# Output projection of a transformer layer as seven block products: low parts of the weights on VectorE, weight sums during the last gates, residual and copies placed early

## The chip, the cores and the metric

The kernel runs on one core of a Trainium2 chip. The metric is the time of one execution on the device in microseconds (us). The engines are named as in the profile: PE (TensorE, matrix products), DVE (VectorE), ACT (ScalarE), POOL (GpSimd) and SP (SyncE, which here only issues DMA transfers). Each engine takes its instructions strictly in the order of its own queue; an instruction that waits holds all that stand behind it on that engine.

## What is computed

One layer over 1024 tokens of width 1024, with 256 context tokens: a modulation from the conditioning vector; a windowed attention (branch A) and a global one (branch B) of 8 heads each; two sigmoid gates; a merge and an output projection; a residual with layer norm; then a convolutional feed-forward block with a second layer norm.

```python
h = x * (1.0 + scale1) + shift1
proj = h @ w_in + b_in
g_a, g_b = split(sigmoid(proj[..., OFF_GA:]), 2)
merged = g_a * (o_a @ w_branch_a) + g_b * (o_b @ w_branch_b)
y = merged @ w_out                                    # the output projection
x = layer_norm(alpha * x + gate1 * y, ln1_g, ln1_b)   # layer norm 1
h = x * (1.0 + scale2) + shift2
u = conv3(h @ w_up) + conv_b
x = layer_norm(alpha * x + gate2 * ((silu(u_gate) * u_val) @ w_down), ln2_g, ln2_b)
```

All is float32. A matrix product is made of three: each operand is split into a high part (rounded to the format that TensorE multiplies) and a low part (the rest), and high x high, high x low and low x high are added up in PSUM (`mm3`, L89 to L92). ACT makes the high part mostly (L82), another engine the low one by a subtraction (L87).

## The kernel before

Tiles are feature-major: 128 features by 1024 tokens. The stages, in order of the profile: query projections, gates, key and value projections and modulation (to about 340 us); 32 attention units (16 of branch A, then 16 of branch B) with the branch A products filled in; the branch B products (tile b) with the merges; the output projection (tile y, 771 to 899 us); the up projection (u and after it the block products a to d); the down projection and layer norm 2.

**The seven block products.** The output projection is a 2 x 2 block product of w_out (transposed) with the merged activations, done with seven half-size products in place of eight. Their order is `WSEQ = 1, 2, 6, 7, 4, 5, 3`. Each product p has two groups g, and each group two halves a, so that `wprod(p, g)` (L1394) gives two results of 128 x 512, each of 4 x 3 matmuls; product 3 does its columns in two slices of 256. Products 2, 4 and 3 add onto the PSUM banks of products 1, 7 and 5 (`WFROM`), so they must wait until those banks have been read. Three PSUM tiles of two banks ("big") go round.

What follows each product:

- Product 1: ACT copies the four results to SBUF (wx, L1424).
- Product 2: DVE adds gate1 times the result onto the residual (`gacc`, L1381; z holds alpha * x); then `zadd` adds z and its square onto the running sums zs (L1218) and zq (L1219) from which layer norm 1 takes mean and variance.
- Product 6: DVE subtracts from wx (L1302), ACT scales the result twice (wy, wx, L1442 and L1443), and POOL adds it at three places (`gsum`, L1388): 12 additions in all.
- Products 7, 4, 5, 3: `gacc` again, and `zadd` where a tile is complete.

The statistics of the first 512 tokens (tile sta, L1250 and L1251) are multiplied in the midst of product 5, by a tick that counts matmul columns; the normalized tiles (B, ACT L1296, zo L1299) feed the up projection.

**Weights.** `wout_load(p)` (L1137) loads the two weight tiles of a product into the raw ring (tag "raw", three buffers; L1152), splits them with ACT and POOL into hwo and lwo, and puts these into one of two rings of four buffers: "w" for products 6, 4 and "wd" for 2, 7, 5; products 1 and 3 have slots of their own. The weights of products 5, 6, 7 and 3 are sums of blocks of w_out, kept in DRAM as wod[1] to wod[4]. They are formed by transfers alone: `wo_put` (L772, issued by SP) copies a block, `wo_acc` (L775, issued by POOL) adds another to it. Each moves 1 MB. A table, `wo_sums`, starts them behind gates: (f = 4) copies 1 and 3, (7) additions to 1 and 3, (9) copy of 1 to 2, (11) addition to 2, (12) copy of 2 to 4, (14) addition to 4. There are 16 gates in two halves each of 24 matmuls; gates 12 to 15 come last, right before the attention.

**Slots.** `ht(name)` takes the oldest free slot (4 KB a partition) from the list `hfree`, and `hput` gives slots back. A tile in a re-used slot waits for the last reader of the tile before it. In the kernel before, wx takes the slots of bT1_7 and bT0_3, the last tiles of the merge, and the first z tiles those of bT0_7 and of the m tiles that product 1 reads.

**The merges.** `merge(f)` (L1098) adds the two branches and splits the result into m; `mbuild(k)` (L1114) forms the differences (bT, L1118) and splits them into W6, W7, W4, W5. These run on DVE, ACT and POOL while TensorE does the branch B products, whose results DVE multiplies by the gate (L1177).

**Who sets the order.** From L1415 on the order on PE is that of the program. On the other engines, and on all in the branch B loop, a planner puts the instructions in order when the kernel is built, from its own estimates of cost and the dependencies; only the sections marked `manual_schedule` are exempt. So the order on DVE, ACT, POOL and SP can differ from the order of the text.

Of the kernel before, what the change touches and what calls it, by code (L numbers as in the profile page):

```python
# [13 lines left out]
P = 128  # L14
# [3 lines left out]
KT = 8  # L18
# [9 lines left out]
HALF = 512  # L28
# [41 lines left out]
def layer_kernel(  # L70
# [600 lines left out]
    def wd_sums(n, j0, j1):  # L671
        def a(r, c):
            return w_dn[c * NH + j0:c * NH + j1][:, :, 4 * r:4 * r + 4].rearrange("n p f q -> p n (f q)")

        def put(key, src, *more):
            tag = tokens.pop()
            t = dpool.tile([P, j1 - j0, HALF], F32, tag=tag, name=f"sd{key}_{j0}")
            for j in range(j0, j1):
                sd[key, j] = t[:, j - j0]
            sd[key] = t  # L680
            nc.sync.dma_start(t, src)
            adds.extend((t, m) for m in more)

        if n == 0:
            put(1, a(1, 0), a(1, 1))
            put(3, a(0, 0), a(1, 0))
        elif n == 1:
            put(2, sd[1], a(0, 0))
        else:
            put(4, sd[2], a(0, 1))  # L690
# [77 lines left out]
    def wo_block(f, c):  # L768
        return w_out[f:f + 4][:, :, 4 * c:4 * c + 4].rearrange("n p k q -> p n (k q)")

    def wo_put(n, src):
        nc.sync.dma_start(wod[n], src)  # L772

    def wo_acc(n, src):
        nc.gpsimd.dma_start(wod[n], src, accum_op=ALU.add)  # L775

    wo_sums = {4: lambda: (wo_put(1, wo_block(4, 0)), wo_put(3, wo_block(0, 0))),
               7: lambda: (wo_acc(1, wo_block(4, 1)), wo_acc(3, wo_block(4, 0))),
               9: lambda: wo_put(2, wod[1]), 11: lambda: wo_acc(2, wo_block(0, 0)),
               12: lambda: wo_put(4, wod[2]), 14: lambda: wo_acc(4, wo_block(0, 1))}  # L780

    sgp = [None]

    def gate(f, hf):
        ps = acc_tile(f"g{f}_{hf}")
        s = slice(hf * HALF, (hf + 1) * HALF)
        for k in range(KT):
            h, l = ready["g", f][k // 4]
            n = slice(k % 4 * P, (k % 4 + 1) * P)
            mm3(ps, (h[:, n], l[:, n]), (hT[k][0][:, s], hT[k][1][:, s]), k == 0, k == KT - 1)  # L790
        if done[0] < total:
            if hf == 0:
                pool, tag = sring[f % 2]
                sgp[0] = pool.tile([P, 2, HALF], F32, tag=tag, name=f"sg{f}", bufs=1)
            sg = sgp[0][:, hf]
        else:
            sg = ph1.tile([P, HALF], F32, tag="sg", name=f"sg{f}_{hf}", bufs=2)
        nc.scalar.activation(sg, ps, AF.Sigmoid, bias=bgc[:, f:f + 1])  # L798
        nc.scalar.dma_start(sgd[f][:, s], sg)
        if hf and f in wo_sums:  # L800
            wo_sums[f]()
        return sg

    queue = [qpost(1, t) for t in range(NT)]
# [188 lines left out]
    for u in range(nu + 1):  # L993
        vs, fs = [], []
        while vq and (vq[0] <= u - VL or vq[0] >= 16 or u >= 17):
            vs += units[vq.pop(0)].value_steps()
        ss = []
        if u < nu:
            ss = units[u].score_steps()
            if u + 2 < nu:  # L1000
                ss.append(units[u + 2].qprep)
        if u == 31:
            first = branch_steps(1, w_b, (0, 1), att, (nc.gpsimd, nc.gpsimd), (0,))
            first[0]()
        for hf, (u0, u1) in enumerate(FILL):
            if u == u0:
                fill += branch_steps(0, w_a, (hf,), att, (nc.gpsimd, nc.gpsimd))
                ends = [n * (u1 - u0) / len(fill) for n in range(len(fill))]
            if u0 <= u < u1:
                fs = [fill.pop(0) for e in ends if u - u0 <= e < u - u0 + 1]  # L1010
        if u < nu:
            ss = [units[u].context] + ss
        seq = []
        for lst, of, sp in ((ss, 0.0, SPAN[u >= 17]), (vs, VOFF, VSPAN), (fs, 0.0, 1.0)):
            for n, st_ in enumerate(lst):
                seq.append((of + sp * (n + 0.5) / len(lst), st_))
        for _, st_ in sorted(seq, key=lambda e: e[0]):
            st_()
        while adds:
            t, m = adds.pop(0)  # L1020
            nc.gpsimd.dma_start(t, m, accum_op=ALU.add)
        if u in DNS:
            wd_sums(*DNS[u])
        if u < nu:
            vq.append(u)
            done(units[u].br, units[u].i, units[u].g)
# [20 lines left out]
    wb = {}  # L1047
# [26 lines left out]
    def hsl(hf):  # L1074
        return slice(hf * HALF, (hf + 1) * HALF)
# [13 lines left out]
    mB, mT = {}, {}  # L1089
    wor = {}  # L1090

    def z_start(f, hf):
        z = zt_[f, hf] = ht(f"z{f}_{hf}", (P, 2, HALF))
        for a in (0, 1):
            nc.sync.dma_start(z[:, a], xT[f + 4 * a][:, hsl(hf)])
        nc.scalar.mul(z, z, ALPHA)

    def merge(f, parts=(0, 1)):  # L1098
# [37 lines left out]

    def wout_load(p, first=False):  # L1137
        pool, tag = ((wq, "w") if WSEQ.index(p) % 2 == 0 else (post, "wd"))
        own = p in (1, 3)
        for g in (0, 1):  # L1140
            if first:
                r = ht(f"rwo{p}_{g}", (P, 2, HALF))
                hput(f"rwo{p}_{g}")
            else:
                r = post.tile([P, 2, HALF], F32, tag="raw", name=f"rwo{p}_{g}", bufs=3)
            src = WSRC[p]
            if type(src) is int:
                src = wod[src][:, 2 * g:2 * g + 2]
            else:
                f, c = src[0] + 2 * g, src[1]  # L1150
                src = w_out[f:f + 2][:, :, 4 * c:4 * c + 4].rearrange("n p k q -> p n (k q)")
            nc.sync.dma_start(r, src)  # L1152
            if own:
                h, l = (ht(f"{a}wo{p}_{g}", (P, 2, HALF), R32) for a in "hl")
            else:
                h, l = (pool.tile([P, 2, HALF], R32, tag=tag, name=f"{a}wo{p}_{g}", bufs=4) for a in "hl")
            split(r, h, l, nc.scalar, nc.gpsimd)
            wor[p, g] = h, l

    for f in (0, 1):  # L1160
        merge(f)
    wb[2] = weight(w_b[2], "wb2", 8, he=nc.scalar, le=nc.vector, rtag=None)
    for f in range(2, KT):
        bT[1, f] = ht(f"bT1_{f}")
        nc.sync.dma_start(bT[1, f], sgd[KT + f])
        w = wb[f // 2]
        halves = [(0, 1)] if f < KT - 1 else [(0,), (1,)]
        for hs in halves:
            n = HALF * len(hs)
            b = bT[1, f][:, hs[0] * HALF:hs[0] * HALF + n]  # L1170
            ps = big(f"b1_{f}") if len(hs) == 2 else sml(f"b1_{f}_{hs[0]}")
            for j in range(4):
                k = (f % 2) * 4 + j
                for m, hf in enumerate(hs):
                    a = O[1, hf, 0, j // 2][:, j % 2], O[1, hf, 1, j // 2][:, j % 2]
                    mm3(ps[:, hsl(m)], (w[0][:, k], w[1][:, k]), a, j == 0, j == 3)
            nc.vector.tensor_tensor(out=b, in0=ps, in1=b, op=ALU.mult)  # L1177
            if len(hs) == 1:
                merge(f, hs)
        if len(halves) == 1:  # L1180
            merge(f)
        if f >= 4:
            mbuild(f - 4)
        if f == 3:
            hput("hwb1", "lwb1")
            wb[3] = weight(w_b[3], "wb3", 8, he=nc.scalar, le=nc.vector, rtag=None)
        if f == 5:
            wout_load(1, True)
    opool.release()

    post = tc.alloc_tile_pool(name="post", bufs=1, side="left", reuse_waits="tile")
# [190 lines left out]
                                       in1=zv(f, s), op0=ALU.mult, op1=ALU.add)  # L1382

    def zadd(f, s, first=False):
        ln_add(zv(f, s), zs, zq, s, first, f"a{f}_{s.start}", nc.vector, nc.vector if s.start and f < 4 else nc.gpsimd)

    def gsum(f, s, src):
        nc.gpsimd.tensor_tensor(out=zv(f, s), in0=zv(f, s), in1=src, op=ALU.add)  # L1388
# [24 lines left out]

    order = ctx.enter_context(ExitStack())
    order.enter_context(tc.manual_schedule(engines={mybir.EngineType.PE}))  # L1415
    def four(n):
        return [t[:, a] for t in [ht(f"w{n}{g}", (P, 2, HALF)) for g in (0, 1)] for a in (0, 1)]

    wx = four("x")
    h0, h1 = hsl(0), hsl(1)  # L1420
    wout_load(2)
    for g in (0, 1):
        for a, o in enumerate(wprod(1, g)):
            nc.scalar.copy(wx[2 * g + a], o)  # L1424
    hput(*[f"m{k}_0" for k in range(4)], *[f"{a}wo1_{g}" for g in (0, 1) for a in "hl"])
    for f in range(4):
        z_start(f, 0)
    wout_load(6)
    for g in (0, 1):
        for a, o in enumerate(wprod(2, g)):  # L1430
# [3 lines left out]
    wout_load(7)  # L1434
    wy = four("y")
    for f in range(4):
        z_start(f, 1)
    for g in (0, 1):
        for a, o in enumerate(wprod(6, g)):
            f = 2 * g + a  # L1440
            sub(nc.vector, wx[f], o, wx[f])
            nc.scalar.activation(wy[f], wx[f], AF.Identity, scale=modc[:, 20 + f:21 + f])  # L1442
            nc.scalar.activation(wx[f], wx[f], AF.Identity, scale=ngain[:, f:f + 1])  # L1443
            gsum(f + 4, h0, wy[f])
            gsum(f + 4, h1, wy[f])
            gsum(f, h1, wx[f])
# [616 lines left out]
```

## Time and profile before

| | us |
|---|---|
| median of 3 runs | 1572.74 |
| lowest, highest | 1570.32, 1573.7 |
| the profiled execution | 1571.2 |
| its span in the profile | 1569.4 |
| output projection, first to last matmul | 771 to 899 |
| last gate ends, attention begins | about 340 |

In the rows of the profile, L12 is line 12 of the kernel. `out<-in` names the tiles without their numbers. A timeline row gives the start, the time from the first start to the last end of the merged instructions, the engine, the line, the operation, its shape and count, and in square brackets how long the engine had stood idle and what ended that. A row of waits reads: who waited for whom, the sum in us, how many times, the longest. A group row gives the least, median and greatest duration in ns, and when the first and the last began. SPq is the queue of transfers that SP issues; its time is that of issuing, not of the transfer.

### The profile page before, as it was taken

The page shows a single profiled execution, that of the slowest core. Times are in us where ns is not written, and L with a number is a line of the kernel's source. Part 1 is how long each engine was busy: PE and PEld are TensorE (multiplying, and loading weights), DVE is VectorE, ACT ScalarE, POOL GpSimd, SP SyncE. Part 2 cuts the span into 40 slices and gives each one's busy share as a digit, 9 for nine tenths or more (in the row PEclk, how much of TensorE's full clock was granted, in tenths as well). Part 3 has the DMA queues.
Part 4 walks back from the last instruction along what each step waited for, and adds up shares of the span by engine and source line. Part 5 has one row for each costly group of instructions (what it writes and reads, how often), then busy time and mean ns, then how long its engine had stood idle before and what let it go on. Part 6 is the DMA issues. An engine that isn't in the chain of part 4 may idle for free.

```text
span 1569.4 us, 22114 instructions
## 1 busy us (share of the span) xinstructions
PE 1514.1 (96%) x7716; PEld 1264.0 (81%) x7716; DVE 1186.0 (76%) x1770; ACT 816.9 (52%) x1352; POOL 816.5 (52%) x754
## 2 busy tenths in 40 slices
PE   9999999999999999999985799999999999999997
PEld 7888877888988888887764798888888888888887
DVE  6676876638988787777944778888888888647884
ACT  5322222449987776665362673544444444435552
POOL 0356522427876777763587445666677664021121
PEclk9999999999999999999988899999999999999998
DMA  9778893313235576644252223233344446996721
GB/s 372 269 238 289 237 320 120 118 64 76 68 102 121 141 175 143 173 102 145 74 194 94 70 79 121 86 117 117 111 102 112 115 115 187 362 261 211 253 101 54
DMA packets 119264, 243.63 MB, mean 155 GB/s; under 512 B 13424, under 2 KB 28272, under 8 KB 119024
## 3 DMA queue, kind: packets, MB, share of 16 engines
q1 hardware_dynamic: 101808, 209.16, 39.7%
q0 software_dynamic: 12512, 24.38, 9.9%
q10 hardware_dynamic: 4832, 8.68, 1.5%
q8 instruction: 60, 0.98, 0.3%
q14 instruction: 52, 0.43, 0.1%
HBM read 190.98 MB, written 74.25 MB: 169 GB/s over the span
## 4 chain that ended last, share of the span: by engine, by line
PE 83%; DVE 4%; DMA 3%; ACT 3%; issue 3%; POOL 2%; SPq 0%; DVEq 0%; ACTq 0%; POOLq 0%
PE ptr L605 4%; PE p L90 4%; PE p L91 4%; PE p L92 4%; PE av L628 4%; PE av L629 3%; PE g L90 3%; PE g L91 3%; PE g L92 3%; PE s L497 3%; PE s L498 3%; PE b L90 2%; PE b L91 2%; PE a L91 2%; PE d L91 2%
## 5 line engine op out<-in xcount | busy, mean ns | idle before, releaser
L548 ACT ACTIVATE p<-p,nm 128x1280 f32<-128x1280 f32 (+2 forms) x128 | 139.8, 1093 | 6.6 <-DVE p L546 6.0
L617 DVE TENSOR_TENSOR ptl<-ptr,pth 128x512 fp32r<-128x512 f32 x195 | 128.1, 684 | 19.9 <-ACT pth L616 17.4
L87 DVE TENSOR_TENSOR ld<-rd,hd 128x1024 fp32r<-128x1024 f32 x77 | 95.6, 1257 | 53.0 <-ACT hd L82 49.3
L616 ACT CAST pth<-ptr 128x512 fp32r<-128x512 f32 x195 | 111.4, 590 | 30.1 <-PE ptr L605 28.1
L82 ACT CAST hd<-rd 128x1024 fp32r<-128x1024 f32 x77 | 79.7, 1047 | 88.7 <-PE p L92 62.5
L605 PEld LDWEIGHTS ptr<-identr,pb 128*128 128x128 f32 x944 | 96.3, 140 | 24.0 <-ACT pb L551 3.1
L605 PE MATMUL ptr<-identr,pb 128*128 128x128 f32 x944 | 107.5, 245 | 1.5 <-ACT pb L551 1.0
L90 PE MATMUL p<-hd 128*128 128x512 f32 x264 | 104.7, 397 | 0.0
L628 PE MATMUL av<-pth,VT 128*128 128x512 f32 x236 | 104.1, 441 | 0.2
L91 PE MATMUL p<-ld,hd 128*128 128x512 f32 x264 | 104.0, 394 | 0.0
L92 PE MATMUL p<-hd,ld 128*128 128x512 f32 x264 | 103.3, 391 | 0.0
L90 PE MATMUL g<-hh,whg 128*128 128x512 f32 x256 | 99.9, 390 | 0.0
L87 POOL TENSOR_TENSOR wlg<-wg,whg 128x512 fp32r<-128x512 f32 x32 | 43.7, 1375 | 108.1 <-ACT whg L82 108.1
L92 PE MATMUL g<-hh,wlg 128*128 128x512 f32 x256 | 99.7, 389 | 0.0
L91 PE MATMUL g<-hl,whg 128*128 128x512 f32 x256 | 99.6, 389 | 0.0
L629 PE MATMUL av<-ptl,VT 128*128 128x512 f32 x236 | 97.4, 413 | 0.2 <-DVE ptl L617 0.2
L546 DVE TENSOR_SCALAR_CACHE_REDUCE p<-s,cvt,nmc 128x1024 f32<-128x1024 f32 x64 | 84.2, 1317 | 5.2 <-PE s L498 5.2
L497 PE MATMUL s<-KL,q 128*128 128x512 f32 (+2 forms) x192 | 73.5, 384 | 1.4 <-DVE p L546 0.9
L798 ACT ACTIVATE sg<-g,bgc 128x512 f32<-128x512 f32 x32 | 22.0, 687 | 96.5 <-PE g L92 91.7
L498 PE MATMUL s<-KL,q 128*128 128x512 f32 (+2 forms) x192 | 71.9, 374 | 0.0
L82 ACT CAST wS<-s 128x512 fp32r<-128x512 f32 x76 | 45.4, 621 | 46.8 <-POOL s L1302 46.8
L82 ACT CAST wA<-ru 128x512 fp32r<-128x512 f32 x57 | 35.4, 621 | 63.3 <-PE d L92 35.3
(457 smaller groups left out, 4982.3 us busy)
## 6 DMA issues: line engine op xcount, KB each, us to landing
wml<-in_wmodT_dram SPq DMA_DIRECT2D x48, 512.0 KB
ru<-in_w_up_dram SPq DMA_DIRECT2D x38, 512.0 KB
rd<-td SPq DMA_DIRECT2D x55, 256.0 KB
rd<-sd SPq DMA_DIRECT2D x44, 256.0 KB
rd<-in_w_dn_dram SPq DMA_DIRECT2D x33, 256.0 KB
wm<-in_wmodT_dram SPq DMA_DIRECT2D x16, 512.0 KB
wg<-in_w_g_dram SPq DMA_DIRECT2D x32, 256.0 KB
sgd<-sg ACTq DMA_DIRECT2D x32, 256.0 KB
```

The source lines that it names most:

```text
L82: nc.scalar.copy(hi, src)
L87: lo_eng.tensor_tensor(out=lo, in0=src, in1=hi.bitcast(F32), op=ALU.subtract)
L90: nc.tensor.matmul(ps, a[0], b[0], start=start, stop=False, skip_group_check=resumed)
L91: nc.tensor.matmul(ps, a[0], b[1], start=False, stop=False, skip_group_check=resumed)
L92: nc.tensor.matmul(ps, a[1], b[0], start=False, stop=stop, skip_group_check=resumed)
L497: nc.tensor.matmul(o, self.q[0][:, hs], ks, start=True, stop=False)
L498: nc.tensor.matmul(o, self.q[1][:, hs], ks, start=False, stop=stop)
L548: nc.scalar.activation(row, row, AF.Exp, bias=self.nm[:, hs], scale=-1.0, accum_out=self.sm[:, hs])
L605: i = nc.tensor.transpose(tr[:, h * P:(h + 1) * P], self.bits[:, h, n * P:(n + 1) * P], identr)
L617: nc.vector.tensor_tensor(out=lo, in0=tr, in1=hi.bitcast(F32), op=ALU.subtract)
L628: nc.tensor.matmul(self.av, v, hi, start=first, stop=False)
L629: nc.tensor.matmul(self.av, v, lo, start=False, stop=self.left == 0)
```

## The change

- The table of weight sums is keyed by gate and half. Copies 1 and 3 go behind gate (12, 0), the additions to them behind (13, 1), the copy of 1 to 2 behind (14, 1), the addition to 2 behind (15, 1). The copy of 2 to 4 goes behind attention unit 1, and the addition to 4 is put on the list that POOL issues at the end of unit 3.
- The split weights of the branch B products 2 and 3 (wb2, wb3) take slots of the free list; product 1's split weights then use the ring "w".
- wx takes its slots before the branch B loop: those of rwb1 and wf1 (counted out by the free list).
- The loads of the first four z tiles are issued in and after the branch B loop (`z_load`). Their slots are then those of hwb2, lwb2, lwb3 and bT0_3. The scaling by alpha (`z_scale`) stays where it was for the first half of the tokens, and for the second half goes into the loop of product 6.
- All 14 low parts of the output weights are made by DVE in place of POOL.
- In the second half of the tokens, the sums zs of f = 4 to 7 are added by DVE in place of POOL (the first, f = 4, is a copy and stays on POOL).

```diff
-    wo_sums = {4: lambda: (wo_put(1, wo_block(4, 0)), wo_put(3, wo_block(0, 0))),
-               7: lambda: (wo_acc(1, wo_block(4, 1)), wo_acc(3, wo_block(4, 0))),
-               9: lambda: wo_put(2, wod[1]), 11: lambda: wo_acc(2, wo_block(0, 0)),
-               12: lambda: wo_put(4, wod[2]), 14: lambda: wo_acc(4, wo_block(0, 1))}
+    wo_sums = {(12, 0): lambda: (wo_put(1, wo_block(4, 0)), wo_put(3, wo_block(0, 0))),
+               (13, 1): lambda: (wo_acc(1, wo_block(4, 1)), wo_acc(3, wo_block(4, 0))),
+               (14, 1): lambda: wo_put(2, wod[1]), (15, 1): lambda: wo_acc(2, wo_block(0, 0))}
...
-        if hf and f in wo_sums:
-            wo_sums[f]()
+        if (f, hf) in wo_sums:
+            wo_sums[f, hf]()
...
+        if u == 1:
+            wo_put(4, wod[2])
+        if u == 2:
+            adds.append((wod[4], wo_block(0, 1)))
...
-    def z_start(f, hf):
+    def z_load(f, hf):
         z = zt_[f, hf] = ht(f"z{f}_{hf}", (P, 2, HALF))
         for a in (0, 1):
             nc.sync.dma_start(z[:, a], xT[f + 4 * a][:, hsl(hf)])
+
+    def z_scale(f, hf):
+        z = zt_[f, hf]
         nc.scalar.mul(z, z, ALPHA)
...
-        own = p in (1, 3)
+        own = p == 3
...
-            split(r, h, l, nc.scalar, nc.gpsimd)
+            split(r, h, l, nc.scalar, nc.vector)
...
-    wb[2] = weight(w_b[2], "wb2", 8, he=nc.scalar, le=nc.vector, rtag=None)
+    def four(n):
+        return [t[:, a] for t in [ht(f"w{n}{g}", (P, 2, HALF)) for g in (0, 1)] for a in (0, 1)]
+
+    wb[2] = weight(w_b[2], "wb2", 8, tag=None, he=nc.scalar, le=nc.vector, rtag=None)
+    wx = four("x")
...
+        if f == KT - 1:
+            hput("hwb3", "lwb3")
...
-            wb[3] = weight(w_b[3], "wb3", 8, he=nc.scalar, le=nc.vector, rtag=None)
+            wb[3] = weight(w_b[3], "wb3", 8, tag=None, he=nc.scalar, le=nc.vector, rtag=None)
         if f == 5:
+            hput("hwb2", "lwb2")
             wout_load(1, True)
+        if f == 6:
+            z_load(0, 0)
+            z_load(1, 0)
+    z_load(2, 0)
+    z_load(3, 0)
...
-        ln_add(zv(f, s), zs, zq, s, first, f"a{f}_{s.start}", nc.vector, nc.vector if s.start and f < 4 else nc.gpsimd)
+        ln_add(zv(f, s), zs, zq, s, first, f"a{f}_{s.start}", nc.vector, nc.vector if s.start else nc.gpsimd)
...
-    hput(*[f"m{k}_0" for k in range(4)], *[f"{a}wo1_{g}" for g in (0, 1) for a in "hl"])
+    hput(*[f"m{k}_0" for k in range(4)])
     for f in range(4):
-        z_start(f, 0)
+        z_scale(f, 0)
...
     for f in range(4):
-        z_start(f, 1)
+        z_load(f, 1)
     for g in (0, 1):
         for a, o in enumerate(wprod(6, g)):
             f = 2 * g + a
             sub(nc.vector, wx[f], o, wx[f])
+            z_scale(f, 1)
```

More of the change, by code (lines that the diff above doesn't have):

```diff
@@ L1415, in layer_kernel @@
     order.enter_context(tc.manual_schedule(engines={mybir.EngineType.PE}))
-    def four(n):
-        return [t[:, a] for t in [ht(f"w{n}{g}", (P, 2, HALF)) for g in (0, 1)] for a in (0, 1)]
-    wx = four("x")
     h0, h1 = hsl(0), hsl(1)
```

## The prediction

> **What bounds the kernel now.** First the busy times on the page, then the view of who waited for whom, for TensorE alone.
>
> ```profile
> PE 1514.1 (96%) x7716; PEld 1264.0 (81%) x7716; DVE 1186.0 (76%) x1770; ACT 816.9 (52%) x1352; POOL 816.5 (52%) x754
> PE y L90 <- DVE z L1381: 12.8, 3, 5.8
> PE sta L1250 <- POOL zs L1218: 11.4, 1, 11.4
> PE y L90 <- ACT wx L1424: 9.5, 1, 9.5
> PE accka L91 <- DVE wlka L87: 4.0, 2, 2.1
> PE sta L1251 <- DVE zq L1219: 0.8, 1, 0.8
> ```
>
> TensorE is the bound: it is busy 96% of the span, so a change pays only where TensorE stands still or runs slowly. The second column of the waits is the sum in us. Four of the five rows belong to the output projection (tile y, statistics sta): 12.8 + 11.4 + 9.5 + 0.8 = 34.5 us. The fifth, 4.0 us, lies far earlier, in the key and value projection (accka). Next, time windows (length, busy times, granted clock, DMA share, GB/s).
>
> ```profile
> 220.00:240.00 20.00, 17.86 (x72) 14.27 (x71) 7.71 (x15) 2.45 (x4) 1.16 (x1) 0.91 0.94 287
> 240.00:260.00 20.00, 18.14 (x73) 14.55 (x72) 11.35 (x34) 5.82 (x12) 6.19 (x6) 0.91 0.37 117
> 320.00:340.00 20.00, 20.00 (x96) 16.55 (x96) 0.00 (x0) 4.06 (x12) 0.21 (x1) 1.00 0.14 53
> 760.00:780.00 20.00, 20.00 (x90) 16.57 (x89) 17.85 (x20) 8.34 (x14) 10.68 (x7) 1.00 0.30 100
> 771.00:899.00 128.00, 93.56 (x413) 78.49 (x411) 73.44 (x94) 65.06 (x92) 86.83 (x54) 0.84 0.38 128
> ...
> L90 PE MATMUL y<-m,hwo x64: 278/389/795, 771.5 to 899.4; 128*128 128x512 f32 x32, 128*128 128x256 f32 x32
> 794.03 0.43 PE y L91
> 797.30 0.23 PE y L91
> ```
>
> The projection occupies 771 to 899 us (its group row: first and last start). TensorE is busy 93.56 of these 128, so 34.4 us are idle, the four waits again. The last two lines, from the chain of work, show a second loss: just after the wait for wx a matmul takes 0.43 us, 3 us later 0.23. Six products of 48 full matmuls and one of 96 half-width ones make 336 full ones, and 336 x 0.23 = 77.3 us. So 128 - 77 = about 51 us are lost: 34.4 idle, some 16 to slow matmuls and the statistics' small ones. In 220 to 260 us TensorE issues 72 + 73 = 145 matmuls where 760 to 780 has 90 in 20 us: 35 too few, at 20/90 = 0.222 us each 7.8 us.
>
> **The change, part by part.** The sum is made against the profiled execution, 1571.2 us (span 1569.4); the median of the three times shown, 1572.74, is 1.5 above it.
>
> *Product 2.* ACT, POOL and DVE around the 9.5 us wait:
>
> ```profile
> 790.19 0.62 ACT L82 CAST W<-bT 128x512 fp32r<-128x512 f32 x1 [3.59 <-POOL bT L1118]
> 790.83 1.07 ACT L1424 COPY wx<-y 128x512 f32<-128x512 f32 x2
> 784.67 2.59 POOL L87 TENSOR_TENSOR lwo<-rwo,hwo 128x1024 fp32r<-128x1024 f32 x1 [2.19 <-ACT hwo L82]
> 788.45 1.71 POOL L1118 TENSOR_TENSOR bT<-bT,bT 128x512 f32<-128x512 f32 x1
> 783.77 0.69 DVE L87 TENSOR_TENSOR m<-bT,m 128x512 fp32r<-128x512 f32 x1
> 803.95 1.41 DVE L1381 SCALAR_TENSOR_TENSOR z<-y,modc,z 128x512 f32<-128x512 f32 x2 [8.44 <-ACT z L1096]
> ```
>
> Product 2 accumulates onto product 1's banks and must wait until wx has been copied out. Product 1 ends about 782.5 (771.5 + 48 x 0.23), but the copy stands on ACT behind a cast that waits for POOL's subtraction at 788.45, which stands behind the low part lwo. The change takes lwo off POOL, and gives wx slots that were free long before (those of rwb1 and wf1, where before they were the last bT tiles'). What is late next: the last m (783.77 + 0.69 = 784.5), then lwo of product 2, now on DVE. Where it is put first, product 2 starts about 786; behind the two or three low parts of W still to come, about 788. I take 4.5 us left of 9.5: **5 saved** (ends 0 and 9.5 plus 2 for the slow start). The z tiles, which came 8.44 us late for DVE at 803.95, must come earlier too, and do: three of the first four load into slots free before product 1 ends (hwb2, lwb2, lwb3), the last waits for bT0_3 until about 793, and is needed at about 798. Nothing is charged.
>
> *The low parts.*
>
> ```profile
> L87 POOL TENSOR_TENSOR lwo<-rwo,hwo x14: 2346/2400/3396, 746.0 to 847.1; 128x1024 fp32r<-128x1024 f32 x14
> L87 DVE TENSOR_TENSOR lwu<-rwu,hwu x6: 1214/1294/3377, 847.2 to 939.6; 128x1024 fp32r<-128x1024 f32 x6
> ACT hwo L82 <- DMA rwo<-wo: 17.6, 2, 9.5
> ```
>
> POOL loses 14 x 2.40 = 33.6 us, DVE takes 14 operations of lwu's shape: between 1.21 and, beside a busy POOL, 3.38 (the 847.18 row below). I take 1.22, because POOL's own lwo, beside which the 3.38 was measured, is gone. That makes 17.1 us, 14.6 of them after 771, where DVE is busy 73.4 of 128 us; they fit. The two of product 1 fall into 740 to 771, where DVE has about a tenth free. Their raw tiles now take the slots of hwb1 and lwb1, free about 750, 21 us before product 1: nothing charged; without that slack a late m would add 2.4 us to the wait of product 2.
>
> *Product 4 and the first statistics.*
>
> ```profile
> 835.78 1.27 POOL L1388 TENSOR_TENSOR z<-z,wx 128x512 f32<-128x512 f32 x1
> 836.76 0.47 PE L90 MATMUL y<-W,hwo 128*128 128x512 f32 x1 [4.07 <-DVE z L1381]
> 816.98 22.75 SPq L1152 DMA_DIRECT2D rwo<-wo  x4
> 841.74 15.67 SPq L1369 DMA_DIRECT2D rwu<-in_w_up_dram  x5
> 847.18 3.38 DVE L87 TENSOR_TENSOR lwu<-rwu,hwu 128x1024 fp32r<-128x1024 f32 x1 [9.25 <-ACT hwu L82]
> 853.82 1.40 DVE L1381 SCALAR_TENSOR_TENSOR z<-y,ngain,z 128x512 f32<-128x512 f32 x2
> 854.71 3.47 POOL L1218 TENSOR_TENSOR zs<-zs,z 128x512 f32<-128x512 f32 x2 [1.35 <-DVE z L1381]
> 858.23 0.59 PE L1250 MATMUL sta<-onec,zs 128*128 128x1 f32 x2 [11.41 <-POOL zs L1218]
> ```
>
> Product 4's second group waits for product 7's last additions, and these for the twelve gsum additions on POOL (12 x 1.27 = 15.2 us), with low parts between them. Without these the sums end some 20 us after product 6 begins (12 matmuls, 2.8, and two short operations, 1.5, before the first, then 15.2), while product 7 ends 22 us after: the wait goes, **4 saved, and 2 of slow clock** (ends 0 and 6). The statistics' wait is a chain: the raw ring has three buffers, freed by POOL's low parts, so SP spreads four loads over 22.75 us; rwu goes out only at 841.74, DVE stands 9.25 us for its cast, and the additions of product 4, queued behind lwu, run at 853.8. Product 4 ended about 842 (836.8 + 24 x 0.23): rwu went out at its end. With the ring freed by DVE it can go out once product 5's weights are split, some 3 us after product 4 begins. What is late next is the plain chain: an addition 0.70, zs on POOL 1.7, against 2.8 us of matmuls before the statistics; I leave 4 us for DVE's queue. Of 12.2 us **8 are saved, and 2** of the slow clock behind (ends 0 and 16).
>
> *Product 3 and the sums of the second half.*
>
> ```profile
> 880.12 1.47 DVE L1218 TENSOR_TENSOR zs<-zs,z 128x256 f32<-128x256 f32 x1 [1.16 <-POOL zs L1218]
> 883.24 0.58 PE L90 MATMUL y<-m,hwo 128*128 128x256 f32 x1 [5.84 <-DVE z L1381]
> 894.51 0.39 PE L90 MATMUL y<-m,hwo 128*128 128x256 f32 x1 [2.91 <-DVE z L1381]
> ```
>
> Three full zs additions go from POOL (1.7) to DVE (0.69, as the m row of that shape). That ends DVE's wait for POOL at 880.12, but here DVE also has the normalization of the first half. 5.84 + 2.91 = 8.75 us of waits: **2 saved**; and since the stage shortens in front of a DVE and ACT load that does not, **3 lost** before the up projection (ends +6 and -6).
>
> *The weight sums.* Before, they run behind gates 4 to 14; the last copy goes out at 222.80.
>
> ```profile
> 222.80 0.51 SPq L772 DMA_DIRECT2D wo<-wo  x1
> 230.20 1.28 DVE L194 CUSTOM_DVE_ANT_0 wml<-wml,scc,bmc 128x1024 f32<-128x1024 f32 x1 [7.33 <-DMA wml<-in_wmodT_dram]
> 232.15 0.50 PE L91 MATMUL accka<-wlka,hh 128*128 128x512 f32 x1 [2.14 <-DVE wlka L87]
> DMA to landing us min/median/max: 11.4/14.2/24.8
> 340.59 0.20 POOL L543 TENSOR_SCALAR p<-sinkb 128x4 f32<-128x4 f32 x1 [2.58 <-PE g L92]
> ```
>
> DVE stood 7.33 us for a modulation weight queued behind a sum's 1 MB copy; wlka came late, and TensorE stopped. The change takes 8 MB of copies and sums out of this stretch, whose DMA share is 0.94. The loss there was 7.8 us: **6 saved** (ends 0 and 7.8). They reappear with the last gates, which end about 340 (p waited for their last matmul); a half gate is 24 matmuls, 5.4 us, so the first copies go out about 302, the first additions about 318, the next copy about 329, where the DMA share is 0.14. POOL's addition into sum 2, due at 340, waits for that copy, and the copy for the first additions; queued behind it are POOL's preparations for the attention (p at 340.59). At the landing of 14.2 the additions land about 333 and the copy about 347: **1 lost**, after some cover (ends 0 and the slower rival below). The last sum goes to attention units 1 to 3: SP's copy stands ahead of query loads, POOL's issue ahead of the next units; nothing charged, as the cover is one unit.
>
> **The sum.** 5 + 6 + 10 + 2 - 3 + 6 - 1 = **25 us**: 1571.2 - 25 = 1546.2, and 1.5 more for the median: **1548**.
>
> **The skill's rule on the clock.** The Trainium skill, "TensorE: Matmul & The Clock Gate" (What's actually happening), says that the clock halves only after an idle window of about 3.4 us. By that rule, waits shortened to 1 to 3 us would cost no slow matmuls, and the sum would be about 3 us better (the better side below holds that). The trace disagrees: the window with the wait of 2.14 us at 232.15 has a clock of 0.91 and 18 matmuls too few, twice what 2.14 us hold.
>
> **The rivals.**
>
> *A, DVE becomes the bound.* For: DVE would have 73.4 + 14.6 + 2 = 90 us of work in the stage, and if each of the 12 low parts also meets a POOL addition (1.27), 105 us, against the 103 that I leave. If the low parts also stand in DVE's queue where ACT's casts waited 17.6 us for loads, the evictions stand with them, and the stage takes 105 + 18 = 123: 5 saved there, 6 - 1 early, 10 in all: 1563. Against: POOL loses the 2.40 us operations, and the loads come earlier as the ring is freed earlier. The Trainium skill, "SBUF — State Buffer" (Who interferes with whom), speaks for A: a VectorE operation with two SBUF inputs and a GpSimd one that reads SBUF exclude each other for a whole instruction. The trace agrees, lwu taking 3.38 us beside POOL's lwo and 1.21 at the least. By that rule each gsum blocks a low part as lwo blocked lwu.
>
> *B, the change doesn't do what it says:* additions on POOL still come last, loads still come late, and TensorE waits as before. For: 12 x 1.27 us of gsum stay. Price 0, with +-3: 1572. Against: the copies' and the ring's chains above both lead through lwo.
>
> *C, slower: POOL's queue stands at the start of the attention.* If each sum and copy lands in the longest time shown, 24.8 us, the additions land at 343, the copy at 368, and POOL's queue stands from 340.6 to 368; TensorE runs out after some 5 us: 22 lost; SP's copy into sum 4 then waits until 393 and holds queries: some 12 more. 34 - 25 = 9 slower: 1582. It decides from landings of about 22 us. Against: 24.8 was measured at a DMA share near 1.
>
> **Chances.** Forecast (1540 to 1556) 0.52; the better side (1533 to 1540, the slow clock and the statistics all won) 0.12; A (1556 to 1567) 0.22; B 0.06; C 0.08. The range 1533 to 1566 leaves out B, C, and little at the ends. What a measurement here tells from no change is 0.2%, 3 us: faster 0.86, same 0.06, slower 0.08.
>
> **What the profile after would show.** Right: TensorE's wait for wx under 5 us, its wait for zs under 5, no wait for wlka; lwo on DVE near 1.22; the stage near 105 us. A: waits of y for DVE's z above 15 us and lwo above 2. C: a wait of TensorE for POOL near 345 us. The forecast falls if low parts standing for casts hold the evictions on DVE, or the up projection waits for B tiles.

## The result and the profile after

The kernel after takes 1560.22 us (median of 4 executions, 1559.57 to 1562.15) against 1573.22 us for the kernel before beside it (4 executions, 1570.32 to 1575.53): a ratio of 0.992, 95% interval 0.9901 to 0.9939. It is faster by 0.8%, 13 us where 25 were forecast. The profiled execution took 1560.66 us, with a span of 1558.7 us, 10.7 us less than before.

The first view is again TensorE's waits (who waited for whom: sum in us, times, longest).

```profile
PE y L90 <- DVE z L1399: 8.7, 2, 5.1
PE accqa L90 <- ACT whqa L82: 8.4, 1, 8.4
PE y L90 <- ACT wx L1438: 6.0, 1, 6.0
PE sta L1268 <- POOL zs L1236: 4.0, 1, 4.0
```

Three rows belong to the output projection; with a fourth of 0.8 us (the zq row in the next timeline) they make 19.5 us where there were 34.5. The wait for wlka is gone. But a wait stands here that the kernel before did not have: accqa, a query projection, for 8.4 us. It is the only one of these rows whose place the change does not seem to touch.

Windows of time (length, busy times with counts for PE, PEld, DVE, ACT, POOL, then granted clock, DMA share, GB/s) show both ends of the account.

```profile
220.00:240.00 20.00, 20.00 (x90) 16.57 (x89) 18.29 (x34) 6.34 (x11) 0.34 (x1) 1.00 0.76 268
240.00:260.00 20.00, 20.00 (x90) 16.57 (x89) 7.33 (x19) 5.97 (x12) 5.23 (x6) 1.00 0.33 99
777.00:889.00 112.00, 92.60 (x417) 78.52 (x416) 87.18 (x108) 64.22 (x91) 59.03 (x39) 0.88 0.39 132
```

From 220 to 260 us TensorE now has 90 matmuls in each 20 us, where it had 72 and 73: the loss beside the weight sums is gone from there. The output projection takes 112 us where it took 128. And yet it starts later: the first matmuls of the stages, from the groups of each tile, stand so (us):

| | before | after |
|---|---|---|
| accqa, first to last | 88.9 to 110.4 | 88.8 to 121.6 |
| accka, first to last | 219.4 to 254.2 | 230.9 to 257.8 |
| last gate matmul | 340.0 | 343.7 |
| attention (s), first | 340.6 | 344.2 |
| output projection (y), first | 771.5 | 776.7 |
| up projection (u), first | 899.9 | 888.8 |

From y to u the kernel gained 128.4 - 112.1 = 16.3 us; up to y it lost 5.2. The rest (0.4) lies behind u. So 11.2 us were lost at accqa, 7.9 won at accka, and 1.6 lost during the attention.

What stood in front of accqa is seen in SP's queue and around it (start, time of issuing). The first fence has SP alone, the second POOL, ACT and PE.

```profile
77.30 0.63 SPq L772 DMA_DIRECT2D wo<-in_w_out_dram  x1
...
84.53 0.57 SPq L772 DMA_DIRECT2D wo<-in_w_out_dram  x1
99.86 0.52 SPq L772 DMA_DIRECT2D wo<-wo  x1
100.47 1.76 SPq L711 DMA_DIRECT2D wqa<-in_w_qa_dram  x3
...
122.75 0.50 SPq L772 DMA_DIRECT2D wo<-wo  x1
```

```profile
87.31 1.38 POOL L775 DMA_DIRECT2D wo<-in_w_out_dram  x1 [11.61 <-DMA wo<-in_w_out_dram]
110.37 0.62 ACT L82 CAST whqa<-wqa 128x512 fp32r<-128x512 f32 x1 [18.06 <-DMA wqa<-in_w_qa_dram]
111.04 0.80 PE L90 MATMUL accqa<-whqa,hh 128*128 128x512 f32 x1 [8.45 <-ACT whqa L82]
```

These are the weight sums. The text puts their entries behind gates 12 to 15, which end after 300 us; SP issues all four copies, the one named behind unit 1 too, between 77 and 123 us. The copy of sum 1 to sum 2 must wait for the addition that POOL issued at 87.31, so SP issues nothing between 85.10 (84.53 + 0.57) and 99.86: 14.8 us (the view of SP's waits puts 14.7 us of waiting to L772, 12.8 of it in one piece, all for transfers into wo). The last three wqa loads stand behind it, ACT's cast waits 18.06 us for them, and TensorE 8.45, with slow matmuls behind.

### The profile page after: what moved, and what is told of

Its sections match the earlier page's. It is cut to its first block, busy times and chain, and to the rows that moved or that the text cites. A ratio compares the mean times of both kernels' runs of the same rounds, so it can differ in the third digit from the quotient of the medians.

```text
span 1558.7 us, 22131 instructions
## 1 busy us (share of the span) xinstructions
PE 1515.0 (97%) x7716; PEld 1265.4 (81%) x7716; DVE 1207.3 (77%) x1787; ACT 817.5 (52%) x1352; POOL 780.6 (50%) x737
## 4 chain that ended last, share of the span: by engine, by line
PE 85%; DVE 5%; DMA 3%; issue 3%; ACT 2%; POOL 2%; SPq 0%; DVEq 0%; ACTq 0%; POOLq 0%
PE ptr L605 5%; PE p L90 4%; PE p L91 4%; PE p L92 4%; PE av L628 4%; PE av L629 3%; PE g L90 3%; PE g L92 3%; PE g L91 3%; PE s L497 3%; PE s L498 3%; PE b L90 2%; PE c L90 2%; PE a L91 2%; PE d L91 2%
```

## Experiments

Ratios are against runs of the kernel before on the same chip, with 95% intervals. Two theories stood at the outset. **Theory 1:** the late start of the output projection comes from the weight sums, because the planner issues them early; a copy depends on no gate, and the text's place is no dependency. **Theory 2:** the sums are harmless, and another edit (slots, early z loads) delays the work before y.

### The sums alone: sums_old and before_sums

sums_old is the kernel after with the old table; before_sums is the kernel before with only the new one.

```diff
# sums_old
-    wo_sums = {(12, 0): ..., (13, 1): ..., (14, 1): ..., (15, 1): ...}
+    wo_sums = {(4, 1): ..., (7, 1): ..., (9, 1): ..., (11, 1): ..., (12, 1): ..., (14, 1): ...}
-        if u == 1:
-            wo_put(4, wod[2])
-        if u == 2:
-            adds.append((wod[4], wo_block(0, 1)))
```

> The changed kernel with the table of weight sums of before (behind gates 4 to 14), all else as changed. Theory 1 (the planner is free to issue the sums once their table entries lie behind the marked section, and issues them at 77 to 130 us, where SP stands for the additions and the query weights come late): TensorE's wait for whqa (8.4) goes, the two waits for wlka (4.0 in all) come back, the first product of y starts at 771.5 as before and not at 776.7, and the time is 1560.2 - 5.2 = 1555. Theory 2 (the late start of y comes from other edits, through new slots or another order): the wait for whqa stays at 8, y starts at 776 to 777, the time is 1560.

> The kernel before with nothing changed but the table of weight sums (and the two entries in the attention units). Theory 1: a wait for whqa of about 8, none for wlka, y starts at 776.7, the projection takes its 128 us, the time is 1573.2 + 5.2 = 1578, slower than before. Theory 2: no wait for whqa, and 1573.

sums_old took 1558.83 us (0.9898, 0.9876 to 0.9921), before_sums 1576.1 us (1.0014, 1.0003 to 1.0025). TensorE's wait in before_sums:

```profile
PE accqa L90 <- ACT whqa L82: 8.8, 1, 8.8
```

The wait at accqa comes with the new table alone and goes with it. The attention's end moves too: y starts at 775.1 us in before_sums against 771.5, and at 773.3 in sums_old against 776.7 after. So the new table costs 2 to 4 us where it was to gain 5; by its times alone before_sums is 2.3 us slower than the kernel before (0.5 to 3.9 by the interval). Each start is that of one profiled execution, and y starts anywhere from 768.8 to 774.7 us in the six kernels with the old table; the last gate matmul parts the runs better: 337.3 to 341.3 us in those six, 343.5 and 343.7 with the new table. Theory 2 falls, though neither time is exactly what theory 1 gave (1555 and 1578): the waits of accka in the profiled run of sums_old (6.5 us, where the kernel before had 4.0) are part of the difference.

### The sums where the text puts them: sums_held

Each copy and each addition gets a dependency on the sigmoid of the gate that the table names, or on unit 1.

```diff
+    hold = [None]
     def wo_put(n, src):
-        nc.sync.dma_start(wod[n], src)
+        i = nc.sync.dma_start(wod[n], src)
+        if hold[0]:
+            tc.add_manual_dep(i.ins, hold[0], data, reason="held")
...
-        nc.scalar.activation(sg, ps, AF.Sigmoid, bias=bgc[:, f:f + 1])
+        hold[0] = nc.scalar.activation(sg, ps, AF.Sigmoid, bias=bgc[:, f:f + 1]).ins.name
```

> The changed kernel, in which each copy and addition also depends on the sigmoid of the gate (or on the unit) behind which the table names it, so that the planner can't issue it earlier. Theory 1: neither a wait for whqa nor for wlka, y starts at 771.5 - 7.8 = 764 unless the attention's start loses something; the time is 1547 to 1549, what the prediction's sum gave. Theory 2: y at 776, 1560. The prediction's rival C: TensorE waits at about 345 us because POOL's queue stands for the addition into sum 2; 2 us at the median landing, up to 30.

It took 1560.01 us (0.9911, 0.9887 to 0.9934): no better than the kernel after. The early part did what was expected: no wait for whqa or wlka, and the last gate matmul at 332.2 us, 7.8 earlier than before. But the attention then took 384.8 us (332.8 to 717.6) against 373.4, so the 1547 to 1549 us of theory 1 did not come. Its beginning, in two views (a window with the columns above, then POOL's and PE's timelines):

```profile
360.00:370.00 10.00, 3.97 (x22) 3.35 (x21) 2.66 (x5) 3.18 (x8) 5.87 (x9) 0.69 0.30 65
```

```profile
333.64 1.15 POOL L779 DMA_DIRECT2D wo<-in_w_out_dram  x1 [19.72 <-ACT sg L803]
...
352.93 1.16 POOL L1026 DMA_DIRECT2D wo<-in_w_out_dram  x1 [0.91 <-DMA wo<-wo]
363.43 0.72 POOL L647 TENSOR_TENSOR ot<-ot,rb 128x256 f32<-128x256 f32 x1 [5.21 <-DMA rb<-dn]
364.50 0.75 PE L605 MATMUL ptr<-identr,pb 128*128 128x128 f32 x4 [3.65 <-ACT rb L574]
```

TensorE is busy 3.97 of 10 us there, where the kernel before had 9.62. POOL does not stand for the sums themselves (0.91 us at 352.93), so that half of rival C does not happen. SP's queue does stand, in two places (two rows of its waits within 328 to 480 us; the last number is the longest wait):

```profile
SPq L579 <- DMA dn<-rb: 17.7, 12, 6.6
SPq L774 <- DMA wo<-in_w_out_dram: 4.7, 1, 4.7
```

The second row is the copy into sum 4, which waits for the addition into sum 2; the second q transfer stands behind it and goes out 14.5 us after the attention's start, where it was 12.3 in the kernel before. That much of rival C came. The first row weighs more: the attention's own small transfer (from rb to dn, which rb is then read from) lands late, while 1 MB sums are moved. In the same stretch of the kernel before, the longest such wait is 1.6 us. POOL then waits 5.21 us for rb, and TensorE 3.65. So the price of the last gates is paid in the attention, at 11.4 us. That the sums in flight make the small transfer late is argued from their times here; the next two runs move them.

### The sums further behind: sums_late and hybrid

sums_late holds all six steps to attention units 2, 4, 6, 8, 10 and 12. hybrid leaves the first lot at the gates (copies 1 and 3 behind gate (12, 0), their additions behind (13, 1)), and holds the other four steps to units 6 to 12.

```diff
-        if u == 1:
-            wo_put(4, wod[2])
-        if u == 2:
-            adds.append((wod[4], wo_block(0, 1)))
+        hold[0] = units[u].owner
+        if u == 6:
+            wo_put(2, wod[1])
+        if u == 8:
+            wo_acc(2, wo_block(0, 0))
+        if u == 10:
+            wo_put(4, wod[2])
+        if u == 12:
+            wo_acc(4, wo_block(0, 1))
```

> As the held sums, but all of them in the attention: copies 1 and 3 behind unit 2, additions behind 4, copy of 1 to 2 behind 6, addition behind 8, copy of 2 to 4 behind 10, addition behind 12, each held to its unit. Theory 1: no wait for whqa or wlka, no wait at the attention's start, y starts at about 764, the time is 1547. Theory 2: 1560. If the additions on POOL delay the units: a wait of TensorE within 360 to 450 us, 2 to 10 us.

> The changed kernel with its sums placed in two lots: the copies and additions of sums 1 and 3 held to the gates that the table names (12 and 13), those of sums 2 and 4 to attention units 6, 8, 10 and 12. Theory 1 (the time of transfer is what counts, and 4 MB between 293 and 332 us cost nothing, while the copies held to units 2 and 4 slowed the attention's start by 5 us): gates end near 332, attention 373 to 376 us, projection from about 766, 1548 to 1551 us. Theory 2 (the attention's start is slowed by whatever the planner puts on SyncE's and GpSimd's queues there, also by the first two additions): as the run with all sums held to units, or worse: attention 379 to 385 us, 1553 to 1560 us.

sums_late took 1553.57 us (0.987, 0.9849 to 0.9891), hybrid 1551.7 us (0.9863, 0.9835 to 0.9892). In sums_late the attention takes 378.8 us, 5.4 more than before, in hybrid 375.9, 2.5 more; in both the gates end at 332. sums_late misses what theory 1 gave it (1547 us, y at about 764): y starts at 769.1. The window of sums_late behind its copies to sums 1 and 3 (issued at 354 and 357 us), in which the first two additions (issued from 370.6) are under way:

```profile
370.00:390.00 20.00, 17.85 (x124) 15.07 (x123) 15.32 (x33) 16.08 (x38) 14.84 (x21) 1.00 0.85 164
```

The DMA share is 0.85, and TensorE is busy 17.85 us where it was 19.96 before. hybrid does these four megabytes before the attention and needs no time for them. That fits theory 1, for which it is the time of the transfers that counts; hybrid's attention is within its range (373 to 376), its time just above it (1548 to 1551). The times alone do not part sums_late from hybrid, since their intervals overlap, and not all of the 5.4 us is the sums': the profile of sums_late is that of its slowest execution (1556.83 us), and its first 20 us of attention, from 330 to 350 us and so before any sum, ran at a granted clock of 0.91.

### The low parts alone, and all but the low parts: before_dvelow and pool_low

```diff
# before_dvelow, in the kernel before
-            split(r, h, l, nc.scalar, nc.gpsimd)
+            split(r, h, l, nc.scalar, nc.vector)
# pool_low, in sums_old
-            split(r, h, l, nc.scalar, nc.vector)
+            split(r, h, l, nc.scalar, nc.gpsimd)
```

> The kernel before (1573.8 us, stage 128.4 us) with one edit: the low parts of the output weights on VectorE. Theory L: nearly the whole gain of the stage, 10 to 15 us, 1559 to 1564 us; the wait for zs under 5 us. Theory S: at most 4 us, 1570 us or more, since the copies still stand behind late slots and VectorE's low parts stand in front of its evictions. If it gains about half (5 to 9 us), both are needed.

> The changed kernel with the old table of the weight sums (as the run with the old sums, 1558.8 us, projection stage 113.8 us) and with the fourteen low parts of the output weights back on GpSimd; the earlier slots and loads, the early residual and the statistics' additions on VectorE stay. Theory L: the low parts carry the stage's gain, since the copies' chain, the raw ring's chain and the late additions all led through them: the stage goes back to 124 to 129 us, the waits for zs and z come back, 1569 to 1574 us. Rival theory S: the earlier slots for wx and for the residual, and zs on VectorE, carry it: the stage stays at 113 to 118 us, 1559 to 1563 us.

before_dvelow took 1558.77 us (0.9915, 0.989 to 0.9939): one word gives the whole gain of the change. pool_low took 1575.44 us (1.0009, 0.9992 to 1.0027): without it nothing is left (theory L had 1569 to 1574 and a stage of 124 to 129). The stage, y to u, is 113.9 us in the first and 131.1 in the second. TensorE's waits, first of before_dvelow, then of pool_low:

```profile
PE y L90 <- DVE z L1381: 8.6, 2, 5.8
PE y L90 <- ACT wx L1424: 7.5, 1, 7.5
...
PE sta L1250 <- POOL zs L1218: 4.1, 1, 4.1
```

```profile
PE sta L1265 <- POOL zs L1233: 12.6, 1, 12.6
PE y L90 <- DVE z L1396: 11.6, 3, 4.5
PE y L90 <- ACT wx L1435: 11.1, 1, 11.1
```

Theory L holds and theory S falls: the statistics' wait (11.4 before) and product 4's follow the engine of the low parts, and of product 2's 9.5 us too 2.0 go by that alone.

### The early slots and the moved additions: zback and zspool

zback is sums_old with the first z tiles loaded, and the slots of wx taken, where the kernel before did so. zspool is sums_old with zs of f = 4 to 7 in the second half back on POOL.

```diff
# zback
-    wx = four("x")
...
-        if f == 6:
-            z_load(0, 0)
-            z_load(1, 0)
-    z_load(2, 0)
-    z_load(3, 0)
...
+    wx = four("x")
...
     for f in range(4):
+        z_load(f, 0)
         z_scale(f, 0)
# zspool
-... nc.vector, nc.vector if s.start else nc.gpsimd)
+... nc.vector, nc.vector if s.start and f < 4 else nc.gpsimd)
```

> The changed kernel with the old table of the weight sums (as the run with the old sums: 1558.8 us, stage 113.8 us, wait for wx 6.0 us), and with the first residual tiles and the slots of wx put back where they were before, at the start of the projection. What stays of the change are the low parts on VectorE, the other slots of the weights and the statistics' additions. Theory L (low parts alone): the stage stays within 2 us, 1557 to 1561 us, and the wait for wx grows by at most 1.5 us, to the 7.5 us of the kernel before with low parts on VectorE. Theory S (the early slots give product 2 its share): the wait for wx goes back to 9 us or more and the residual holds VectorE again: 1562 to 1566 us.

> The changed kernel with the old table of the weight sums (1558.8 us), and with the statistics' additions of the second half for the last four blocks back on GpSimd. The prediction gave these 2 us in product 3. Theory P (as predicted): the waits of y for z in product 3 grow, 1560 to 1562 us. Theory Q (VectorE's queue is what product 3 waits for, so additions moved onto it cost as much as they free): no change or up to 3 us faster, 1556 to 1559 us.

zback took 1558.78 us (0.9909, 0.9895 to 0.9924), zspool 1558.09 us (0.9912, 0.9892 to 0.9931), both within 1 us of sums_old. The stage is 112.9 us in zback and 112.2 in zspool, against 113.9. The waits that each was to bring back, first zback's, then zspool's:

```profile
PE y L90 <- ACT wx L1430: 4.6, 2, 4.2
```

```profile
PE y L90 <- DVE z L1396: 8.7, 2, 5.8
```

With the late slots the wait for wx is shorter (6.0 in sums_old), and with the additions on POOL the wait for z is no longer (9.6 in sums_old). Neither edit earns anything that these runs can tell.

### Product 3 in another order: hybrid_p3

```diff
-    for g in (0, 1):
-        for si in (1, 2):
+    for si in (1, 2):
+        for g in (0, 1):
```

> As the run with the sums in two lots, and product 3 goes through its two 256-column slices one after the other over both groups, where it went group by group over both slices. In the changed kernel two waits of y for VectorE's z stand there, 5.06 and 3.60 us. Theory Q (a bank is wanted again before VectorE's queue has come to its eviction; with twice the distance it has): 4 to 8 us less than the run before it, stage 104 to 109 us. Theory W (VectorE has no time left in that stretch, whatever the order): within 2 us of the run before it, the wait only moves, to the end of the product or to the up projection.

It took 1544.28 us (1543.36 to 1546.14; ratio 0.9818, 0.9783 to 0.9852), 7.4 us less than hybrid (medians, same chip) and the fastest of all that ran. Waits of hybrid, then of hybrid_p3:

```profile
PE y L90 <- DVE z L1410: 11.2, 3, 4.9
```

```profile
PE y L90 <- DVE z L1410: 3.5, 2, 2.1
```

And the stage as a window, again hybrid, then hybrid_p3:

```profile
766.00:879.50 113.50, 91.32 (x418) 77.04 (x417) 87.15 (x108) 64.35 (x91) 58.85 (x39) 0.88 0.39 130
```

```profile
766.00:870.00 104.00, 88.67 (x416) 74.44 (x415) 82.83 (x101) 60.52 (x85) 58.84 (x39) 0.92 0.39 133
```

The stage goes from 113.5 to 104.2 us (the last 0.2 lie behind the window), a little more than the wait loses, since the clock rises from 0.88 to 0.92. Theory Q holds: VectorE's queue came to the evictions of one slice after the next slice wanted the bank, and with the other order it comes early enough. The 87.15 of 113.5 us are an average over the stage and do not speak against theory W: in product 3 itself VectorE is busy 23.34 of 26.8 us in hybrid (852.7 to 879.5) and all 17.7 us in hybrid_p3 (852.5 to 870.2). So the order earned 7 us, and now VectorE is what fills that stretch.

## Why the prediction was right and wrong, step by step

**The step that failed is the weight sums.** "They reappear with the last gates, which end about 340" read a place in the text as a time, and gave 6 saved and 1 lost, +5. Measured up to the first y: 5.2 lost, 10 us of the 14 by which the span missed the forecast (one profile on each side; the times of before_sums put the loss at 2.3). The first half was right: the wait at accka and its 7.9 us went. The sums reappeared at 77 to 123 us, in front of another projection's weights, because nothing that they depend on held them (sums_held, with such a dependency, has them from 295 us on). The prediction worked out landings from gates without asking what ties a transfer to its gate, and the profile before could have told it. There too the sums do not run "behind gates 4 to 14": its own row at 222.80 is the copy named behind gate 12, and the addition named behind gate 14 follows at 229.02, while the sigmoids of gates 12 to 15 run from 302.66 to 341.15 us.

```profile
229.02 1.16 POOL L775 DMA_DIRECT2D wo<-in_w_out_dram  x1 [17.47 <-DMA wo<-wo]
```

The "1 lost" was wrong as well: tied to the gates as told, they cost 11.4 us in the attention (sums_held). Placed in the attention (sums_late) they give +2.4, and in two lots (hybrid) +5.5 (y at 766.0 against 771.5), close to the +5 of the sum.

**Statistics: right.** 8 were to go and 4 to stay; 11.41 became 4.00. Both this row and the next are from the timeline of the kernel after.

```profile
846.86 0.58 PE L1268 MATMUL sta<-onec,zs 128*128 128x1 f32 x2 [4.00 <-POOL zs L1236]
848.21 0.58 PE L1269 MATMUL sta<-onec,zq 128*128 128x1 f32 x2 [0.76 <-DVE zq L1237]
```

**Product 4: right.** Its wait of 4.07 us has no row any more. Both went through the low parts, as the steps had it (before_dvelow, pool_low).

**Product 2: too high.** 5 were to go; 9.5 became 6.0, 3.5. ACT and DVE in front of it:

```profile
791.53 1.04 ACT L82 CAST hwo<-rwo 128x1024 fp32r<-128x1024 f32 x1
792.60 1.07 ACT L1438 COPY wx<-y 128x512 f32<-128x512 f32 x2
```

```profile
791.45 0.68 DVE L1113 SCALAR_TENSOR_TENSOR m<-bT,m 128x512 fp32r<-128x512 f32 x1
...
792.12 1.21 DVE L87 TENSOR_TENSOR lwo<-rwo,hwo 128x1024 fp32r<-128x1024 f32 x1
```

Product 1 ended about 788, and the copy stands behind casts until 792.60. The prediction put product 2's start "behind the two or three low parts of W still to come"; here the last m and the first lwo, at 791 and 792, are as late as the copy. From 780 to 800 us DVE is busy 19.94 of 20 us. That its queue sets this start is argued from these rows and was not tried. The reason by slots was wrong: with the old slots the wait is 4.6 (zback), and what the low parts do by themselves is 2.0 (before_dvelow).

**Product 3: nothing.** 2 were to go; 5.84 + 2.91 = 8.75 became the two z rows below, 5.06 + 3.60 = 8.66. The prediction looked for POOL's share in VectorE's queue; zspool shows no gain from it (its waits there are 8.7 us, in sums_old 4.63 + 4.55, and its time cannot tell 2 us), hybrid_p3 that the order of the slices is worth 7.

**The tail: too dark.** 3 were to be lost before the up projection. u follows y at once (888.7, 888.8), and only 0.4 is lost behind it.

**Slow matmuls: too high.** 2 + 2 us were to go with the waits. The stage gained 16.3, its waits 34.5 - 19.5 = 15.0, so about 1.3 came from the clock (0.84 to 0.88 in the stage's windows). The waits that stayed are still long enough to slow what follows:

```profile
871.14 0.58 PE L90 MATMUL y<-m,hwo 128*128 128x256 f32 x1 [5.06 <-DVE z L1399]
...
883.47 0.39 PE L90 MATMUL y<-m,hwo 128*128 128x256 f32 x1 [3.60 <-DVE z L1399]
```

So the stage was to give 5 + 6 + 10 + 2 - 3 = 20 us and gave 16.3; the sums were to give 5 and took 5.2.

**The rivals.** The time lies in A's bounds (1556 to 1567), but A is not what happened: lwo took 1.22 us in the median and 2.31 at most, and the stage 112 us, not 123. Its case was overstated, too: the "103 that I leave" takes all 25 us off the stage's 128, though 5 of them (6 - 1) lie before it; the prediction's own parts leave 105 to 108, which A's 105 us of work on VectorE do not exceed. B is excluded by the stage's 16 us. C named the right place; but in sums_held POOL's queue did not stand, SP's stood for 4.7 us, the price was 11.4 us and not 34, and in the kernel after the planner had moved the sums away from the attention. Of the signs that were named for being right, the wait for zs, wlka and lwo came as said; the wait for wx (6.0, not under 5) and the stage (112, not 105) did not.

## What to carry over

A line's place in the program is not its time: before an instruction that depends on nothing is given a time, ask what holds it there, and for a transfer on an in-order queue also what it will hold. If it is to be late, make it depend on what is late, and then look at what small transfers it meets there. When a change has several parts, run the cheapest part by itself first; here one word of it carried the whole gain, and a change of loop order that was not in it gave 7 us more.

## What the runs showed of the hardware

**What follows a short wait.** In hybrid_p3, product 3's waits of 2.10 and 1.38 us are followed at once by matmuls at full pace; in the kernel after, the wait of 3.60 us at 883.47 is followed by five quick matmuls and then by slow ones. hybrid_p3 first, then the kernel after:

```profile
860.53 0.39 PE L90 MATMUL y<-m,hwo 128*128 128x256 f32 x1 [2.10 <-DVE z L1410]
...
860.99 0.28 PE L90 MATMUL y<-m,hwo 128*128 128x256 f32 x1
861.11 0.28 PE L91 MATMUL y<-m,hwo 128*128 128x256 f32 x1
```

```profile
884.16 0.40 PE L92 MATMUL y<-m,lwo 128*128 128x256 f32 x1
884.36 0.41 PE L90 MATMUL y<-m,hwo 128*128 128x256 f32 x1
884.57 0.41 PE L91 MATMUL y<-m,hwo 128*128 128x256 f32 x1
```

The starts lie 0.12 us apart in the first, 0.21 in the second. The Trainium skill, "TensorE: Matmul & The Clock Gate" (What's actually happening), has the clock halve after an idle window of about 3.4 us; these two places agree. Two others do not. In the kernel before, the waits of 2.14 and 1.86 us at accka are each followed, some matmuls later, by about eight that start 0.43 us apart where 0.23 is usual. And in hybrid_p3 the up projection begins with about eight such matmuls (from 870.56 us; granted clock 0.66 from 870 to 875), though no wait in product 3 before them is longer than 2.10 us. So the short waits were not free there; u's first to last matmul take 2.5 us longer than in hybrid:

```profile
L90 PE MATMUL u<-B,hwu x120: 276/388/486, 879.5 to 947.3; 128*128 128x512 f32 x72, 128*128 128x256 f32 x48
```

```profile
L90 PE MATMUL u<-B,hwu x120: 275/388/628, 870.2 to 940.5; 128*128 128x512 f32 x72, 128*128 128x256 f32 x48
```

So of the 9.3 us by which hybrid_p3's stage is shorter, only 7.4 are left in its time. What decides whether slow matmuls follow is not shown by these runs: the prediction's dismissal of the rule went too far, and one idle stretch of 3.4 us does not account for all four places either.

**The sums' additions land sooner where the DMA share is lower.** The four additions of 1 MB took 14.2 us to landing in the median and 24.8 at most in the kernel before, where the DMA share was 0.94 from 220 to 240 us. In hybrid they are spread over the last gates and the attention, with a share of 0.77 from 311 to 332 us and 0.74 from 430 to 445:

```profile
DMA to landing us min/median/max: 8.9/10.0/14.9
```
